# One layer of a hybrid mLSTM and attention backbone: the root of the mLSTM head norms as a power on GpSimd, and the last head's masks moved

## The chip, the cores and the metric

The kernel runs on one core of one Trainium2 chip. The metric is the device time of one execution in microseconds (us), the median of several runs. Engines: PE is TensorE's matrix multiply and PEld its weight load, DVE is VectorE, ACT is ScalarE, POOL is GpSimd, SP is SyncE, which issues the DMAs here.

## The reference, cut to what matters

One layer, 1024 latent tokens and 256 context tokens of width 1024. After a modulated norm and one input projection there are two groups of heads, a bidirectional mLSTM (4 heads of 128) and a windowed attention; their outputs are joined, projected, and followed by a gated convolutional mixer. The change lies in the mLSTM group:

```
d_log = cum[..., :, None] - cum[..., None, :] + li[..., None, :]
order = tril(ones((MLSTM_CHUNK, MLSTM_CHUNK)))
d_log = where(order, d_log, -inf)              # the mask
m_t = maximum(a_log, max(d_log, axis=-1))
dec = exp(d_log - m_t[..., None])              # the decay
s = einsum('bhntd,bhnsd->bhnts', q, k) * dec
...
def mlstm_merge(h, o, gain):                   # the head norm
    hn = h * rsqrt(mean(h * h, axis=-1) + EPS)
    return hn * gain * sigmoid(o)
```

## The kernel before

Tokens are worked on in blocks of 128: 2 context blocks (NC) and 8 latent blocks (NL). The four mLSTM heads (H = 4) go one after the other. While the recurrence of head h runs (`mlstm(h, ...)`), the dense projections of head h + 1 (`dense`) are interleaved with it, piece by piece: the outer loop takes one step of the recurrence and then as much dense work as a rate allows. Beside the last head there is no next one; there the query projections of attention (`qgen`, tile px) are interleaved, at a lower rate, and what is left of them runs after the head.

For one head, `mlstm` does the following.

- It loads `ee` (8 blocks of 128 x 2 x 128, both directions) by four broadcast DMAs from DRAM, two blocks each (`ee_load`, line 659). `ee` has one buffer, so the first load waits for the last use by the head before.
- Nine backward states, i = 0 to 8: transposes of the keys (line 665, tile pn, four buffers), two scaled copies on ScalarE (lines 669, 671), a product (line 692), and the state update on VectorE (line 700 for the first, 702 for the others), which releases pn. In between it adds the masks to `ee` (`mask(b)`, line 675; `mask(i - 2)` from i = 2, the last one with the first forward state) and takes the exponentials (`decay(b)`, line 679). At i = 7 the output gate is formed (lines 715, 716).
- Forward states and outputs by block: scores (line 734) times `ee` (line 737), forward state (722, 727), products with the states and values (745, 746, 748), division by the normaliser (751 to 760), and on line 763 a square with a running sum into `hss[:, b]`.
- `finish()`: a root of `hss` on ScalarE (796), its inverse on VectorE (797), and for each block the scale of the head's output into `ym` (799). For heads 0 to 2 it is a generator that the next head's backward states step through from i = 1 on (`next(fins[0])`): the root, the inverse and block 0 in the first step, a block in each later one. For the last head it runs whole at the end.

ScalarE's functions come from tables. Tanh (566, 715) and Exp (679, 1152) run without a reload between them; Sqrt needs another one. So each root brings a table load before it (at line 796) and another before the next Tanh or Exp (566 in heads 1 and 2, 679 in the last head, 1044 after it).

The order of work: in the stages of heads 0 to 2 (the recurrence of head h with the projections of head h + 1) the order on every engine is as written. In the stage of the last head only TensorE's order is as written; what VectorE, ScalarE, GpSimd and the DMA queue do is put in order by the framework's planner when the program is built, by its own estimates of when each instruction is ready, with the order of writing as the priority. After the last head, memory of the recurrence is freed and given to attention's tiles (`kT2`, `vv`, `wor`); an Exp on one element of `vv` (line 1044) and the loads of `vv`'s raw values (line 927, wor<-kv_d) come first there. GpSimd has no work between the input stage and attention.

Of the kernel before, what the change touches and what calls it, by code (L numbers as in the profile page):

```python
# [12 lines left out]
AF = mybir.ActivationFunctionType  # L13
ALU = mybir.AluOpType
# [9 lines left out]
NL = SEQ // P  # L24
NC = CTX // P
NCH = NL + NC
H = 4
DH = 128
# [6 lines left out]
EPS = 1e-6  # L35
# [43 lines left out]
def build(tc, I, out, dbg=None):  # L79
    nc = tc.nc  # L80
    dbg = dbg or {}
    V, S, G, T = nc.vector, nc.scalar, nc.gpsimd, nc.tensor
# [11 lines left out]
    eps_t = cp.tile([P, 1], F32, name="eps_t")  # L94

    def spc(n, i=0, w=1):
        a = SP[n][0] + i
        return sp[:, a:a + w]

    def rwc(n, i=0, w=None):  # L100
        a, b = RW[n]
        return rw[:, a + i:(b if w is None else a + i + w)]
# [81 lines left out]
    tri = xp.tile([P, 2, P], F32, name="tri", bufs=1)  # L184
# [458 lines left out]
            dump("kT", kT[:]); dump("qT", qT[:]); dump("va", va[:].rearrange("p c e -> p (c e)"))  # L643

    fins = []

    def mlstm(h, kT, qT, va):
        cbk = tp.tile([P, NL, DH + 1], F32, name="cbk", tag="cbk", bufs=1)
# [2 lines left out]
        hss = tp.tile([P, NL], F32, name="hss", tag="hss")  # L651
        g1 = lambda t, d, c: t[:, d, c, h:h + 1]
        yv = ym[:, :, h * DH:(h + 1) * DH]
        E1 = DH + 1


        ee = tp.tile([P, NL, 2, P], F32, name="ee", tag="ee", bufs=1)
        def ee_load(b):
            nc.sync.dma_start(ee[:, b:b + 2], m_d[:].rearrange("(c h) d t -> h c d t", h=H)
                              [h:h + 1, NC + b:NC + b + 2].broadcast_to([P, 2, 2, P]))  # L660

        ee_load(0)
        def tr(c):
            pn = pl.tile([P, 512], F32, name="pn", tag="l")
            T.transpose(pn[:, 0:P], kT[:, c * P:(c + 1) * P], ident[:])
            kwb = None
            if c != NC:
                kwb = tp.tile([P, DH], F32, name="kwb", tag="kwb", bufs=3)
                S.activation(kwb[:], pn[:, 0:P], AF.Copy, scale=g1(gw, 1, c))
            if c < NCH - 1:  # L670
                S.activation(kwf[:, c], pn[:, 0:P], AF.Copy, scale=g1(gw, 0, c))
            return pn, kwb

        def mask(b):
            V.tensor_tensor(out=ee[:, b], in0=ee[:, b], in1=tri[:], op=ALU.add)

        def decay(b):
            for d in range(2):
                S.activation(ee[:, b, d], ee[:, b, d], AF.Exp, bias=g1(a_, d, NC + b), scale=-1.0)
# [6 lines left out]
        for i, c in enumerate(order[1][:-1]):  # L686
            pn, kwb = ahead.pop(0)
            if i + 2 < NCH - 1:
                ahead.append(tr(order[1][i + 2]))
            elif i + 2 == NCH - 1:  # L690
                tr(order[1][i + 2])
            T.matmul(pn[:, P:P + E1], kwb[:], va[:, c], start=True, stop=True)
            if c == 1:
                nx = tp.tile([P, E1], F32, name="cst", tag="cst")[:]
            elif c == 0:
                nx = cbk[:, NL - 1]
            else:
                nx = cbk[:, c - NC - 1]
            if prev is None:
                V.tensor_copy(nx, pn[:, P:P + E1])  # L700
            else:
                V.scalar_tensor_tensor(out=nx, in0=prev, scalar=g1(gd, 1, c), in1=pn[:, P:P + E1],
                                       op0=ALU.mult, op1=ALU.add)
            prev = nx
            if i < 3:
                ee_load(2 * i + 2)
            if fins and i:
                next(fins[0])
            if i > 1:
                mask(i - 2)  # L710
            if i in (4, 6, 8):
                decay(i // 2 - 2)
            if i == TN:

                S.activation(yv, yv, AF.Tanh, scale=0.5)
                V.scalar_tensor_tensor(out=yv, in0=yv, scalar=1.0, in1=rwc("gain", h * DH, DH).unsqueeze(1)
                                       .broadcast_to([P, NL, DH]), op0=ALU.add, op1=ALU.mult)
            yield
        cf, cfs = [None], []

        def step(c, ps):
            T.matmul(ps, kwf[:, c], va[:, c], start=True, stop=True)
            nx = tp.tile([P, E1], F32, name="cst", tag="cst")
            if cf[0] is None:
                V.tensor_copy(nx[:], ps)
            else:
                V.scalar_tensor_tensor(out=nx[:], in0=cf[0], scalar=g1(gd, 0, c), in1=ps, op0=ALU.mult, op1=ALU.add)
            cf[0] = nx[:]
            cfs.append(nx[:])

        def first(c):
# [3 lines left out]
            if b:  # L735
                step(c - 1, pe[:, P:P + E1])
            V.scalar_tensor_tensor(out=ee[:, b], in0=pe[:, 0:P].unsqueeze(1).broadcast_to([P, 2, P]),
# [29 lines left out]
        for c in range(NC):  # L767
            pn = pl.tile([P, 512], F32, name="pn", tag="l")
            step(c, pn[:, 0:E1])
            if c == 0:  # L770
                cfs.clear()
            if c == 0:
                mask(NL - 1)
            decay(3 + c)
            yield
        first(NC)
# [16 lines left out]
        cfs.clear()  # L793

        def finish():
            S.activation(hss[:], hss[:], AF.Sqrt, bias=eps_t[:], scale=1.0 / DH)
            V.reciprocal(hss[:], hss[:])
            for b in range(NL):
                V.scalar_tensor_tensor(out=yv[:, b], in0=hid[:, b], scalar=hss[:, b:b + 1], in1=yv[:, b],
                                       op0=ALU.mult, op1=ALU.mult)  # L800
                if b < NL - 1:
                    yield
            fins.clear()
            yield
        if h < H - 1:
            fins.append(finish())
        else:
            for _ in finish():
                pass
# [179 lines left out]
    for h in range(H):  # L989
# [20 lines left out]
        with tc.manual_schedule(engines=order_):  # L1010
            dn = dense(h + 1, wkq, wvo, *nh) if nh else qgen()
            rate = RATE if nh else RATE3
            for n, _ in enumerate(mlstm(h, *cur)):
                if nh is None and n == LW3:
                    late()
                    rga = pq.tile([P, D], F32, name="rga", tag="rga")
                    nc.sync.dma_start(rga[:], row(0))
                if nh and n in (2, LW):
                    w = wnext((n // LW,))
                    if n == LW:  # L1020
                        wvo.append(w)
                        wnext = ahead_load(h + 2, 0)
                elif nh and n in (24, 27):
                    wkq = wnext((n // 27,))
                    if n == 27 and h + 2 < H:
                        wnext = ahead_load(h + 2, 1)
                elif nh and n >= 3 and n != 15:
                    next(ada, 0)
                debt += rate * (1 + (n == 0))
                while debt > 0:  # L1030
                    w = next(dn, None)
                    if w is None:
                        break
                    debt -= w
# [1003 lines left out]
    for t, (p, ps, fresh) in enumerate(products):  # L2038
        for j in range(NP):
# [35 lines left out]
            if NP + 3 <= n < NP + 3 + NL:  # L2075
                b = n - NP - 3
# [118 lines left out]
```

## Time and profile before

| | |
|---|---|
| median of 3 runs | 1264.26 us (1264.09 to 1265.34) |
| the profiled execution | 1263.85 us |
| its span | 1262.1 us |
| granted TensorE clock, mean | 0.999 |
| TensorE busy | 1233.2 us (98%) |
| VectorE busy | 973.4 us (77%) |
| ScalarE busy | 638.8 us (51%) |
| GpSimd busy | 187.5 us (15%) |
| ScalarE's table loads at line 796 | 4, 1283 ns each |

The span runs from the first to the last instruction of one profiled execution, the time of an execution also has what lies around it. Rows of a time line give the start in us, the duration in us, the engine, the line, the operation, out<-in, the shapes and the count of instructions that were merged; in brackets stands how long the engine was idle before it and what ended that wait. In the groups by line the columns are busy us and mean ns, then the idle time before them.

### The profile page before, as it was taken

Reading aid. Unit: us, or ns where it says so; the run is one execution under the profiler, and the core shown is the slowest. Engines: PE = TensorE matmul, PEld = TensorE weight load, DVE = VectorE, ACT = ScalarE, POOL = GpSimd, SP = SyncE. Lnnn points to the kernel's source line nnn. Section 1 sums busy time; section 2 is a strip of 40 time slices with the busy share of each in tenths; the row PEclk is TensorE's granted clock in tenths of the full one; section 3 lists DMA queues with packets and bytes.
Section 4 is the critical chain, followed back from the end, with each engine's and each line's share of the span. In section 5 each row is a group of like instructions: output and inputs, shape, how many; then the busy total and the mean of one; then the engine's idle time right before and its main releaser. Section 6 shows DMA issues by size and latency. Waiting matters only on the chain.

```text
span 1262.1 us, 19247 instructions
## 1 busy us (share of the span) xinstructions
PE 1233.2 (98%) x7044; PEld 1059.5 (84%) x7044; DVE 973.4 (77%) x1691; ACT 638.8 (51%) x1310; POOL 187.5 (15%) x162
## 2 busy tenths in 40 slices
PE   6999999999999999999999999999999999999997
PEld 4799999999898888888887888888888888788886
DVE  5863777777887888788987877777777777877887
ACT  6732556464865777776843333333333334434435
POOL 1200000000001444221002232133231232001000
PEclk9999999999999999999999999999999999999999
DMA  9541635352254333104314322223322237975563
GB/s 360 190 138 35 151 117 152 119 178 68 85 176 165 128 126 110 51 34 167 117 51 133 116 98 104 93 101 116 103 105 100 94 136 269 335 252 187 192 195 134
DMA packets 90560, 176.17 MB, mean 140 GB/s; under 512 B 12954, under 2 KB 29538, under 8 KB 90466
## 3 DMA queue, kind: packets, MB, share of 16 engines
q1 hardware_dynamic: 90178, 174.15, 41.1%
q8 instruction: 56, 0.92, 0.3%
q10 hardware_dynamic: 288, 0.79, 0.2%
q14 instruction: 38, 0.31, 0.1%
HBM read 136.58 MB, written 38.33 MB: 139 GB/s over the span
## 4 chain that ended last, share of the span: by engine, by line
PE 80%; DVE 7%; ACT 5%; DMA 5%; issue 2%; SPq 1%; POOL 1%; ACTq 0%; DVEq 0%; POOLq 0%
PE pd L2032 14%; PE pa L1492 8%; PE pc L1492 8%; PE pp L600 7%; PE pe L1492 4%; PE pd L1492 4%; PE pb L1492 4%; PE u L1194 3%; PE pv L305 2%; PE pv L307 2%; PE pv L306 2%; DMA wa<-in_w_ada_dram 2%; PE pt L1171 2%; PE po L305 2%; PE po L307 1%
## 5 line engine op out<-in xcount | busy, mean ns | idle before, releaser
L1609 ACT CAST wh<-Rb 128x1024 fp32r<-128x1024 f32 (+1 forms) x63 | 56.8, 903 | 144.4 <-PE pd L1492 77.3
L2032 PE MATMUL pd<-dh,al 128*128 128x512 f32 x296 | 115.4, 390 | 0.8 <-DVE al L1373 0.8
L2032 PE MATMUL pd<-dl,ah 128*128 128x512 f32 x296 | 115.3, 389 | 0.0
L2032 PE MATMUL pd<-dh,ah 128*128 128x512 f32 x296 | 115.2, 389 | 0.0
L1492 PE MATMUL pc<-hB,wh 128*128 128x512 f32 x344 | 105.5, 389 | 0.0
L1492 PE MATMUL pa<-hB,wh 128*128 128x512 f32 x336 | 103.7, 390 | 0.3 <-ACT sn L1691 0.2
L1210 DVE TENSOR_TENSOR wl<-Rb,wh 128x1024 fp32r<-128x1024 f32 (+1 forms) x63 | 65.8, 1046 | 39.2 <-ACT wh L1609 38.6
L1727 POOL TENSOR_TENSOR tt<-vt,tt 128x512 f32<-128x512 f32 x22 | 29.5, 1343 | 367.5 <-ACT tt L1721 367.5
L600 PE MATMUL pp<-hl,wh 128*128 128x512 f32 x256 | 79.3, 405 | 0.0
L305 PE MATMUL pv<-wh,hl 128*128 128x256 f32 x256 | 75.9, 296 | 0.0
L1492 PEld LDWEIGHTS pc<-hB,wh 128*128 128x128 f32 x344 | 64.6, 188 | 13.4
L1492 PEld LDWEIGHTS pa<-hB,wh 128*128 128x128 f32 x336 | 62.9, 188 | 14.0 <-ACT sn L1691 1.1
L307 PE MATMUL pv<-wh,hl 128*128 128x256 f32 x256 | 72.4, 283 | 0.0
L306 PE MATMUL pv<-wl,hl 128*128 128x256 f32 x256 | 72.3, 282 | 0.0
L1492 PE MATMUL pc<-hB,wl 128*128 128x512 f32 x172 | 66.4, 389 | 0.0
L2032 PEld LDWEIGHTS pd<-dh,al 128*128 128x128 f32 x296 | 55.6, 188 | 12.9 <-DVE al L1373 1.6
L2032 PEld LDWEIGHTS pd<-dl,ah 128*128 128x128 f32 x296 | 55.6, 188 | 12.0 <-DVE dl L1373 0.3
L1492 PE MATMUL pa<-hB,wl 128*128 128x512 f32 x168 | 65.4, 389 | 0.0
L2032 PEld LDWEIGHTS pd<-dh,ah 128*128 128x128 f32 x296 | 55.6, 188 | 11.6
L1178 ACT CAST ph<-pt 128x512 fp32r<-128x512 f32 (+1 forms) x88 | 46.2, 525 | 26.0 <-PE pt L1171 25.8
L1148 DVE TENSOR_REDUCE nm<-sps 128x1 f32<-128x641 f32 (+1 forms) x64 | 50.3, 786 | 4.9 <-PE sps L1144 3.4
L1492 PE MATMUL pd<-hB,wh 128*128 128x512 f32 x176 | 53.9, 390 | 0.0
(1095 smaller groups left out, 3692.1 us busy)
## 6 DMA issues: line engine op xcount, KB each, us to landing
w<-in_w_ada_dram SPq DMA_DIRECT2D x64, 256.0 KB, 2.7
br<-in_w_down_dram SPq DMA_DIRECT2D x25, 512.0 KB, 5.6
ar<-act_s SPq DMA_DIRECT2D x44, 256.0 KB, 3.2
Ra<-in_w_up_dram SPq DMA_DIRECT2D x21, 512.0 KB, 3.6
Rb<-in_w_up_dram SPq DMA_DIRECT2D x21, 512.0 KB, 3.6
act_a<-tt SPq DMA_DIRECT2D x33, 256.0 KB, 2.0
act_s<-tt SPq DMA_DIRECT2D x33, 256.0 KB, 2.0
wr<-in_w_h_dram SPq DMA_DIRECT2D x16, 512.0 KB, 5.1
```

The costliest lines, as they stand in the source:

```text
L305: T.matmul(ps, st_hi, mv_hi, start=first, stop=False)
L306: T.matmul(ps, st_hi, mv_lo, start=False, stop=False)
L307: T.matmul(ps, st_lo, mv_hi, start=False, stop=last)
L600: T.matmul(pp[:, 512 * n:512 * n + 512], wkq[sw][:, kt, cs], hl[n][part][:, kt, :], start=kt == 0 and sw + part == 0, stop=kt == KT - 1 an ...
L1148: V.tensor_reduce(out=self.nm[:, j:j + 1], in_=self.sv[j], axis=AX.X, op=ALU.max, negate=True)
L1178: S.copy(self.ph[i][:, :w], self.pt[i][:, :w])
L1194: T.matmul(self.u[:], vv[:, c, self.g], part[i][:, kk * 2 * P:(kk + 1) * 2 * P], start=kb + m == 0, stop=kb == last and m == 1)
L1210: sub = lambda e, o, x, y: e.tensor_tensor(out=o, in0=x, in1=y, op=ALU.subtract)
L1492: T.matmul(ps[:, cols], wt[sw][:, j, kt * P:kt * P + P], hB[part][:, blk, kt, cols], start=first and n == 0, stop=last and n == len(seq) - ...
L1609: S.copy(wt[0][:], src)
L1727: G.tensor_tensor(out=self.tt[:, h2_], in0=self.vt[:], in1=self.tt[:, h2_], op=ALU.mult)
L2032: T.matmul(ps[:], ac[sa][:, js], w[sw], start=first and n == 0, stop=last and n == 2, skip_group_check=not fresh)
```

## The change

The root and the inverse become two instructions on GpSimd: a multiply-add of `hss` (times 1/128, plus EPS), and a power with exponent -0.5, taken from a small constant tile. That constant is written once before the heads, over eight columns of `bsh_a`, a parameter that is not read any more by then. With it the Sqrt table is no longer needed by the four heads.

In the last head (`lag` = 3 instead of 1), masks are written two states later: `mask(i - 4)` from i = 4 on, and masks 5, 6 and 7 with the first forward state. Its masks of blocks 0 and 1 run on GpSimd instead of VectorE. In heads 0 to 2 the masks stay as they are.

```
     fins = []
+    G.memset(spc("bsh_a", 0, NL), -0.5)
...
+        lag = 1 if h < H - 1 else 3
...
         def mask(b):
-            V.tensor_tensor(out=ee[:, b], in0=ee[:, b], in1=tri[:], op=ALU.add)
+            e = G if lag > 1 and b < 2 else V
+            e.tensor_tensor(out=ee[:, b], in0=ee[:, b], in1=tri[:], op=ALU.add)
...
-            if i > 1:
-                mask(i - 2)
+            if i > lag:
+                mask(i - lag - 1)
...
-            if c == 0:
-                mask(NL - 1)
+            for b in (range(NL - lag, NL) if c == 0 else ()):
+                mask(b)
...
         def finish():
-            S.activation(hss[:], hss[:], AF.Sqrt, bias=eps_t[:], scale=1.0 / DH)
-            V.reciprocal(hss[:], hss[:])
+            G.tensor_scalar(out=hss[:], in0=hss[:], scalar1=1.0 / DH, scalar2=EPS, op0=ALU.mult, op1=ALU.add)
+            G.tensor_tensor(out=hss[:], in0=hss[:], in1=spc("bsh_a", 0, NL), op=ALU.pow)
```

## The prediction

> **What bounds the kernel now.** I read the page first, for the busy shares.
>
> ```profile
> span 1262.1 us, 19247 instructions
> PE 1233.2 (98%) x7044; PEld 1059.5 (84%) x7044; DVE 973.4 (77%) x1691; ACT 638.8 (51%) x1310; POOL 187.5 (15%) x162
> ```
>
> TensorE is busy for 1233.2 of 1262.1 us, so the change can win only where TensorE waits. The next view is the busy time by stretch (columns: PE, PEld, DVE, ACT, POOL, granted clock, DMA share, GB/s), around the last head, which runs from 320.7 to about 394 us.
>
> ```profile
> 300.00:320.00 20.00, 20.00 (x173) 20.00 (x172) 14.03 (x35) 11.31 (x35) 0.00 (x0) 1.00 0.03 10
> 320.00:340.00 20.00, 18.30 (x145) 16.68 (x144) 16.95 (x56) 17.88 (x54) 0.00 (x0) 1.00 0.38 107
> 340.00:360.00 20.00, 19.14 (x169) 18.91 (x168) 16.57 (x65) 14.70 (x45) 0.00 (x0) 1.00 0.21 73
> ```
>
> Up to 320 us TensorE has no idle time; between 320 and 360 us it idles 1.70 + 0.86 = 2.56 us, with VectorE and ScalarE fuller than before. GpSimd does nothing in any of the three, and the clock is at 1.00. So the size of any gain is about 2.6 us plus what stands behind 360 us, out of 1264.26: 0.2%, or 2.53 us, which is about what a measurement of this kernel can tell from no change.
>
> The third view is the chain of waits, with the start of each head's dense stage (first key matmuls) and the one extra block of TensorE work.
>
> ```profile
> 123.89 2.88 PE pc__1499 L592 x24
> 188.96 2.88 PE pc__2268 L592 x24
> 226.46 0.79 PE pq L831 x8
> 254.90 2.88 PE pc__3055 L592 x24
> ```
>
> Head 0's stage takes 188.96 - 123.89 = 65.07 us and has no norm of an earlier head to finish; head 1's takes 254.90 - 188.96 = 65.94 us and has one, besides the block of 0.79 us at 226.46. That leaves 0.08 us for a whole finish with its two table loads, root and inverse.
>
> **Part 1, the root in heads 0 and 1.** Each finish drops a table load, a root and an inverse, and the load that restores the table. ScalarE's order of time, and VectorE's row that comes after the inverse:
>
> ```profile
> 190.57 0.19 ACT L763 ACTIVATION_READ_ACCUMULATOR nm<-hid 128x1 f32 x1
> 197.24 1.28 ACT L796 ACT_TABLE_LOAD   x1
> 198.53 0.30 ACT L796 ACTIVATE hss<-hss,eps_t 128x8 f32<-128x8 f32 x1
> 199.10 0.35 DVE L799 SCALAR_TENSOR_TENSOR ym<-hid,hss,ym 128x128 f32<-128x128 f32 x1
> ```
>
> By the 0.08 us above this is worth nothing: all engines keep their order here, and TensorE has no gap to close. I put it at 0, with ends of 0 and -0.2 (two heads at 0.08). What covers the new work: the sums of squares are complete at 190.76, the scale on line 799 runs at 199.10, so the two GpSimd instructions have 8.3 us. If that cover were gone, line 799 would hold back VectorE's queue, with the state updates (line 702) behind it, and TensorE behind those.
>
> The Trainium skill, "ScalarE: Activation LUTs", section "What ACT_TABLE_LOAD costs", counts a drain of about 1.38 us on top of the load, about 2.66 us a switch. Here the root starts at 198.53, right where the load of 1.28 us ends, so this trace shows no drain in the price. By the page each removed load would free twice the ScalarE time; my sum would stay, since ScalarE does not set the end in it.
>
> What do the two GpSimd instructions cost? The page's groups have these rows.
>
> ```profile
> L908 POOL TENSOR_TENSOR wor<-wor,rga 128x512 f32<-128x512 f32 x8 | 10.3, 1288 | 2.5 <-DMA wor<-in_w_out_dram 2.5
> L2184 POOL MEMSET const-bfloat16-1.0<- 128x1 bf16 x1 | 0.1, 102 | 0.0
> ```
>
> On 8 elements a multiply-add should be near the memset, 0.1 us. No row has a power. From below it is 0.1 us, from above I take 1.8 us, more than any two-input row of its engine above; my value is 1.0 us, in the middle, as neither row is like it. The same memset row prices the new constant, once, on an engine that is idle: 0.
>
> **Part 2, the last head's front.** Three views of the same time: VectorE, ScalarE, TensorE.
>
> ```profile
> 322.12 0.35 DVE L760 SCALAR_TENSOR_TENSOR hid<-nm,dn,hid 128x128 f32<-128x128 f32 x1 [0.53 <-ACT hid L759]
> 323.80 0.76 DVE L675 TENSOR_TENSOR ee<-ee,tri 128x256 f32<-128x256 f32 x2 [1.32 <-DMA ee<-m_d]
> 324.47 0.29 DVE L700 COPY cst<-pn 128x129 f32<-128x129 f32 x1
> 325.02 0.76 DVE L675 TENSOR_TENSOR ee<-ee,tri 128x256 f32<-128x256 f32 x2 [0.26 <-DMA ee<-m_d]
> 325.70 0.34 DVE L702 SCALAR_TENSOR_TENSOR cbk<-cst,gd,pn 128x129 f32<-128x129 f32 x1
> 327.69 0.19 DVE L797 RECIPROCAL hss<-hss 128x8 f32<-128x8 f32 x1
> 327.80 0.30 DVE L702 SCALAR_TENSOR_TENSOR cbk<-cbk,gd,pn 128x129 f32<-128x129 f32 x1
> 339.00 0.43 DVE L752 TENSOR_TENSOR nm<-pi,nm 128x258 f32<-128x258 f32 x1 [0.32 <-PE pe L734]
> 341.05 1.23 DVE L157 TENSOR_TENSOR wl<-wr,wh 128x1024 fp32r<-128x1024 f32 x1 [0.23 <-ACT wh L156]
> 344.31 0.42 DVE L737 SCALAR_TENSOR_TENSOR ee<-pe,ee 128x256 f32<-128x256 f32 x1
> ```
>
> ```profile
> 324.63 1.28 ACT L796 ACT_TABLE_LOAD   x1
> 328.56 1.28 ACT L679 ACT_TABLE_LOAD   x1
> ```
>
> ```profile
> 324.82 0.33 PE L665 MATMUL pn<-ident,kT 128*128 128x128 f32 x1 [0.43 <-DVE cst L700]
> 330.38 0.33 PE L665 MATMUL pn<-ident,kT 128*128 128x128 f32 x1 [0.30 <-DVE cbk L702]
> 331.11 0.49 PE L692 MATMUL pn<-va,kwb 128*128 128x129 f32 x2 [0.40 <-ACT kwf L671]
> 344.87 0.35 PE L745 MATMUL pj<-cst,qT 128*128 128x129 f32 x1 [0.86 <-DVE ee L737]
> ```
>
> VectorE waits for the broadcast loads of ee: 1.32 us before blocks 0 and 1 and 0.26 us before blocks 2 and 3. From 325.02 on its rows follow without a gap but for 0.32 and 0.23 us until line 737 at 344.31, which releases TensorE's longest stall, 0.86 us. So from 325.02 to 344.7 VectorE's list of work sets the time. What ScalarE or TensorE get done earlier in between only moves TensorE's stall to 344.
>
> *Blocks 0 and 1 to GpSimd.* VectorE loses 324.47 - 323.80 = 0.67 us of masks ahead of the first state's copy (line 700), and the copy no longer waits for the load. TensorE's 0.43 us at 324.82 goes. What is late next: masks 2 and 3, which wait for the second load until 325.02 and stand ahead of line 702.
>
> *The lag.* In the text of the kernel before, masks 2 and 3 belong to states 4 and 5, yet they sit ahead of state 1's update (325.70). The planner, not the text, put them there, because VectorE had nothing else ready. Writing them two states later leaves them as ready as before, so I expect them in the same place: 0. At the other end they go behind, and VectorE is free of the waits and of the moved masks: 1.32 + 0.67 + 0.26 = 2.25 us. I stay with 0, since the planner has already moved them three states forward. On GpSimd a mask has half the elements of line 908's row, so about 0.65 to 1.29 us; both are done by 326.4, and block 0 is first read by ScalarE's exponential, behind the load at 328.56. Masks 5 to 7 end up after the first forward state, the same work in the same stretch: 0.
>
> *The inverse* leaves VectorE at 327.69: the next row starts 0.11 us later, so -0.1. *The two gaps* of 0.32 and 0.23 us may close when TensorE and ScalarE are ahead: between 0 and -0.55, I take -0.3. *The two table loads* are 2.56 us of ScalarE; the second stands in the chain ahead of TensorE's stalls at 330.38 and 331.11 (0.70 us). With VectorE as the bound they give 0, at most -0.7.
>
> **Part 3, the last head's end.** ScalarE, VectorE, TensorE:
>
> ```profile
> 356.12 0.20 ACT L763 ACTIVATION_READ_ACCUMULATOR nm<-hid 128x1 f32 x1
> 357.94 0.30 ACT L796 ACTIVATE hss<-hss,eps_t 128x8 f32<-128x8 f32 x1
> ```
>
> ```profile
> 358.69 2.18 DVE L799 SCALAR_TENSOR_TENSOR ym<-hid,hss,ym 128x128 f32<-128x128 f32 x8
> ```
>
> ```profile
> 371.93 0.51 PE L895 MATMUL pt<-identr,qs 128*128 128x128 f32 x4 [0.38 <-DVE qs L890]
> ```
>
> The sums are ready at 356.32, the root at 358.24. On GpSimd 0.1 + 1.0 us give the power at 357.4, up to 0.8 us sooner. The eight scales free the room into which the values of attention are loaded, and the chain leads through those loads and VectorE to TensorE's 0.38 us at 371.93. I take -0.3, between 0 and -0.38. The load for Exp after it goes too, under query projections that keep TensorE busy: 0.
>
> **Sum.** 0 - 0.1 - 0.3 - 0.3 = -0.7 us. The profiled execution took 1263.85 us (span 1262.1 and 1.75 around it), so 1263.15; it lies 0.41 us under the median of the runs, 1264.26, which makes the forecast 1263.5 us.
>
> **Rivals.** *The lag works* (masks 2 and 3 leave the head of VectorE's list): -0.7 - 2.25 = -2.95 us, which is also all of the 2.56 + 0.38 us that TensorE idles: 1261.3. For it: the longest waits of the front are these loads. Against: those two masks ran ahead of the text before.
>
> *The ports.* Two VectorE groups of the same operation and size differ where GpSimd works beside one of them:
>
> ```profile
> L1210 DVE TENSOR_TENSOR Rb<-Rb,Ra 128x512 f32<-128x512 f32 x21 | 32.0, 1525 | 0.7
> L1210 DVE TENSOR_TENSOR Rb<-Ra,Rb 128x512 f32<-128x512 f32 x42 | 28.1, 710 | 0.0
> ```
>
> That is 0.82 us for one instruction. If GpSimd's two masks slip to where VectorE adds masks 2 and 3, each holds one of them up by as much: at most 1.6 us, and about 1.1 with half-sized masks; the forecast becomes 1264.6, no change. Against: the first load lands at 323.80, when VectorE has nothing to mask. The Trainium skill, "SBUF — State Buffer", section "SBUF: two separate sides", says that a VectorE instruction with two SBUF inputs and a GpSimd one exclude each other for a whole instruction; the two rows agree with it.
>
> *The power is slow.* From 356.32 it may take 1.9 us before it is later than the root; past that each us delays the scales, the loads and the stall at 371.93 one for one. At 6 us the loss there is about 4.1 us and the result 1264.26 - 0.4 + 4.1 = 1268.0, slower; it becomes a measurable loss from about 4.8 us on. The 8.3 us of heads 0 and 1 would still cover it. For it: no row prices the power. Against: no GpSimd instruction of the rows above goes past 1.3 us, with 512 elements and not 8.
>
> **Chances.** The forecast 0.50, on its own 1262.5 to 1264.3; the lag works 0.22; the ports 0.15; the slow power 0.07; another order of VectorE's or the DMA queue's work through the planner, either way, 0.06. Faster by over 0.2% means under 1261.7: two thirds of the second case and half of the last, 0.18. Slower means over 1266.8: 0.07, with the slow power. Within: 0.75. The range, 1261.0 to 1265.4, leaves out the slow power, a third of the lag's case and some of the last.
>
> **What would show it.** Right: TensorE at 100% and the stage lengths of heads 0 and 1 unchanged; no table load at lines 679 and 1044; line 700 near 322.9; masks 2 and 3 still waiting for their load ahead of the first line 702; a stall at line 745 that remains. Wrong: line 702 ahead of all VectorE masks; VectorE masks of about 1 us; a wait for GpSimd at line 799.

## The result: slower by 0.4%

| | before | after |
|---|---|---|
| median of 6 runs each, same chip | 1264.38 us | 1268.99 us |
| ratio, 95% interval | | 1.0038 (1.0028 to 1.0048) |
| the profiled execution, its span | 1262.1 us | 1267.2 us |

The forecast was 1263.5 us and no change; the change costs 4.6 us. The head of the page after:

```profile
span 1267.2 us, 19257 instructions
PE 1234.8 (97%) x7044; PEld 1059.8 (84%) x7044; DVE 972.4 (77%) x1685; ACT 628.0 (50%) x1298; POOL 196.5 (16%) x173
```

VectorE and ScalarE have 1.0 and 10.8 us less work, as the change wants, GpSimd has 9.0 us more, and the span is 5.1 us longer. TensorE's busy time, with the same 7044 matmuls, is only 1.6 us higher, so most of the loss is waiting. The window in which most of it stands:

```profile
320.00:340.00 20.00, 15.30 (x122) 14.08 (x121) 14.57 (x45) 14.39 (x47) 3.29 (x4) 1.00 0.42 107
```

Between 320 and 340 us TensorE idles 4.70 us where it idled 1.70. The second measure is a shift: the start of each TensorE instruction less that of the same one in the kernel before, as the median over a stretch. From 40 to 318 us it is 0.10 us and constant (this shift of the start differs from kernel to kernel below, from -0.27 to 1.51 us). From 324 to 327 us it falls by 0.6 to 0.9, a gain; by 345 to 358 us it is 2.10 us above the start (the **front** of the last head), by 392 to 420 us another 1.94 (the **end**), and by 1150 us another 1.01. These three make the 5.1 us with the start. Heads 0 and 1, by the starts of the same key matmuls in the chain of waits after:

```profile
123.99 2.88 PE pc__1500 L592 x24
189.06 2.88 PE pc__2269 L592 x24
255.00 2.88 PE pc__3056 L592 x24
```

The stages are 65.07 and 65.94 us long, to the hundredth what they were.

What the new instructions cost, by the groups after (busy us and mean ns):

```profile
L800 POOL TENSOR_TENSOR hss<-hss,sp 128x8 f32<-128x8 f32 x4 | 6.6, 1649 | 0.3
L799 POOL TENSOR_SCALAR hss<-hss 128x8 f32<-128x8 f32 x4 | 0.8, 200 | 227.4 <-DMA w<-in_w_ada_dram 132.2 <-ACT nm L766 95.1
L678 POOL TENSOR_TENSOR ee<-ee,tri 128x256 f32<-128x256 f32 x2 | 1.4, 740 | 65.5 <-ACT kwb L671 65.5
```

A power is 1.65 us and a mask 0.74, inside the bounds of the prediction (0.1 to 1.8 and 0.65 to 1.29); a multiply-add is 0.20, twice what it was put at. No new instruction is far from its price; what the 1.65 us of the power cost where they stand is tested below. Line numbers after are those of before plus 2 for lines 665 to 671 and plus 3 behind them (675 is 678, 702 is 705, 737 is 740, 745 is 748, 799 is 802, 908 is 911). The kernels below that keep a root in some heads have four lines more behind line 801 (802 is 806, 893 is 897, 911 is 915).

The front after, first GpSimd and VectorE (start, duration, engine, line; in brackets the wait):

```profile
324.28 1.44 POOL L678 TENSOR_TENSOR ee<-ee,tri 128x256 f32<-128x256 f32 x2 [65.45 <-ACT kwb L671]
325.80 0.20 POOL L799 TENSOR_SCALAR hss<-hss 128x8 f32<-128x8 f32 x1
326.08 1.65 POOL L800 TENSOR_TENSOR hss<-hss,sp 128x8 f32<-128x8 f32 x1
```

```profile
323.00 0.29 DVE L703 COPY cst<-pn 128x129 f32<-128x129 f32 x1 [0.43 <-PE pn L695]
324.52 0.35 DVE L705 SCALAR_TENSOR_TENSOR cbk<-cst,gd,pn 128x129 f32<-128x129 f32 x1
327.76 0.35 DVE L802 SCALAR_TENSOR_TENSOR ym<-hid,hss,ym 128x128 f32<-128x128 f32 x1 [2.90 <-POOL hss L800]
328.03 0.34 DVE L705 SCALAR_TENSOR_TENSOR cbk<-cbk,gd,pn 128x129 f32<-128x129 f32 x1
331.64 0.42 DVE L678 TENSOR_TENSOR ee<-ee,tri 128x256 f32<-128x256 f32 x1
335.75 1.21 DVE L157 TENSOR_TENSOR wl<-wr,wh 128x1024 fp32r<-128x1024 f32 x1
338.22 0.41 DVE L740 SCALAR_TENSOR_TENSOR ee<-pe,ee 128x256 f32<-128x256 f32 x1
```

The first state is copied at 323.00, as foretold, and VectorE's first mask comes only at 331.64, behind six state updates: the lag has moved the masks. But the planner gave GpSimd the two masks first and head 2's power behind them. The masks' load is issued at 320.22 and takes 3.6 us to land, and the masks start at 324.28 (the bracket names a copy of ScalarE that ended just ahead of that; with the masks alone, in run e2, it names the load). And the planner put the scale of line 802 ahead of the second state update. VectorE stands for 2.90 us with that update behind it. ScalarE and TensorE in the same time:

```profile
331.27 1.05 ACT L156 CAST wh<-wr 128x1024 fp32r<-128x1024 f32 x1 [1.00 <-DMA wr<-in_w_q_dram]
332.23 0.36 ACT L671 ACTIVATE kwb<-pn,gw 128x128 f32<-128x128 f32 x1
```

```profile
328.43 0.33 PE L667 MATMUL pn<-ident,kT 128*128 128x128 f32 x1 [1.87 <-DVE cbk L705]
332.90 0.49 PE L695 MATMUL pn<-va,kwb 128*128 128x129 f32 x2 [0.64 <-ACT kwf L673]
338.69 0.71 PE L751 MATMUL pi<-va,ee 128*128 128x129 f32 x4 [1.59 <-DVE ee L740]
```

A second thing is new on ScalarE, the place of the cast of attention's query weight (line 156). ScalarE and VectorE before:

```profile
332.04 0.37 ACT L671 ACTIVATE kwf<-pn,gw 128x128 f32<-128x128 f32 x1
334.05 1.05 ACT L156 CAST wh<-wr 128x1024 fp32r<-128x1024 f32 x1
```

```profile
334.67 0.43 DVE L737 SCALAR_TENSOR_TENSOR ee<-pe,ee 128x256 f32<-128x256 f32 x1
335.13 1.22 DVE L157 TENSOR_TENSOR wl<-wr,wh 128x1024 fp32r<-128x1024 f32 x1
```

The cast ran at 334.05 before, behind all scaled copies of the backward states; now it stands ahead of the last one's (332.23) and waits for its load. The load is not later: it is issued at 325.44 and takes 5.7 us to land, against 325.32 and 5.9 us before. And on VectorE the cast's other half (line 157, 1.21 us) now stands ahead of the first score multiplication, line 740, for which TensorE waits 1.59 us.

The end after, ScalarE's last sum, GpSimd, VectorE, TensorE:

```profile
358.63 0.20 ACT L766 ACTIVATION_READ_ACCUMULATOR nm<-hid 128x1 f32 x1
```

```profile
359.19 1.64 POOL L800 TENSOR_TENSOR hss<-hss,sp 128x8 f32<-128x8 f32 x1
```

```profile
360.87 2.19 DVE L802 SCALAR_TENSOR_TENSOR ym<-hid,hss,ym 128x128 f32<-128x128 f32 x8 [1.87 <-POOL hss L800]
376.44 1.23 DVE L911 TENSOR_TENSOR wor<-wor,rga 128x1024 f32<-128x1024 f32 x1 [0.42 <-DMA wor<-in_w_out_dram]
378.74 1.23 DVE L911 TENSOR_TENSOR wor<-wor,rga 128x1024 f32<-128x1024 f32 x1 [0.41 <-DMA wor<-in_w_out_dram]
```

```profile
374.87 0.52 PE L898 MATMUL pt<-identr,qs 128*128 128x128 f32 x4 [0.59 <-DVE qs L893]
382.91 0.50 PE L898 MATMUL pt<-identr,qs 128*128 128x128 f32 x4 [1.00 <-DVE qs L893]
```

Before, VectorE had a query to rotate while the root ran:

```profile
357.95 0.42 DVE L317 TENSOR_TENSOR ta<-px,rope 128x256 f32<-128x256 f32 x1 [0.87 <-PE px L307]
358.40 0.38 DVE L317 TENSOR_TENSOR z<-px,rope 128x256 f32<-128x256 f32 x1
```

Now it waits 1.87 us for the power, and later two scalings of w_out stand close together, each waiting for its load, ahead of the rest of a query (line 893) for which TensorE waits. One wait of 0.38 us has become 0.59 and 1.00.

### The profile page after: what moved, and what is told of

It is laid out like the page before. It is cut to its first block, busy times and chain, and to the rows that moved or that the text cites. A ratio compares the mean times of both kernels' runs of the same rounds, so it can differ in the third digit from the quotient of the medians.

```text
span 1267.2 us, 19257 instructions
## 1 busy us (share of the span) xinstructions
PE 1234.8 (97%) x7044; PEld 1059.8 (84%) x7044; DVE 972.4 (77%) x1685; ACT 628.0 (50%) x1298; POOL 196.5 (16%) x173
## 4 chain that ended last, share of the span: by engine, by line
PE 77%; DVE 9%; ACT 5%; DMA 5%; issue 2%; SPq 1%; POOL 1%; DVEq 0%; ACTq 0%; POOLq 0%
PE pd L2035 12%; PE pa L1495 8%; PE pc L1495 8%; PE pp L600 7%; PE pe L1495 4%; PE pd L1495 4%; PE pb L1495 4%; PE u L1197 3%; PE pv L305 2%; PE pv L307 2%; PE pv L306 2%; PE pt L1174 2%; PE po L305 2%; PE po L307 1%; PE po L306 1%
```

## The experiments

Each kernel was measured in 5 rounds beside the kernel before. An engine's **list** is the order of its instructions. The shifts are those of the one profiled execution, each stretch less the one ahead of it; the last column is VectorE's wait for GpSimd at the scales of the last head's own end. "Late" is everything behind 420 us; where it is large it arises mostly between 600 and 630 us; half of the change's comes at 1070.

How far a shift of one execution can be trusted, the kernels with equal lists show. e14 and e15 have the change's list on every engine and on the DMA queue: their late parts are 0.19 and 0.11 us where the change has 1.01 (e10 and e16, again with one list, have 2.75 and 1.11), so much of "late" is scatter between executions. Up to the last head's end e15 is the change, instruction for instruction, and its front is 3.17 where the change has 2.10; e2 and e3, equal up to there as well, are 0.07 us apart.

| kernel | median, before | ratio (95%) | front | end | late | wait at end |
|---|---|---|---|---|---|---|
| the change | 1268.99, 1264.38 | 1.0038 (1.0028, 1.0048) | 2.10 | 1.94 | 1.01 | 1.87 |
| e1 power alone | 1268.64, 1264.56 | 1.0029 (1.0018, 1.0040) | 0.58 | 1.51 | 2.71 | 1.87 |
| e2 masks alone | 1265.05, 1264.56 | 1.0005 (0.9996, 1.0014) | -0.88 | 1.21 | 0.33 | none |
| e4 root at the end | 1268.13, 1264.56 | 1.0034 (1.0021, 1.0046) | 2.17 | 0.79 | 1.30 | none |
| e5 power first in GpSimd's queue | 1269.61, 1264.56 | 1.0040 (1.0028, 1.0053) | 2.28 | 2.44 | 0.05 | 1.88 |
| e3 root in the front | 1266.19, 1264.91 | 1.0012 (1.0003, 1.0021) | -0.81 | 2.69 | 0.39 | 1.96 |
| e9 power in heads 0, 1 alone | 1265.74, 1264.91 | 1.0006 (0.9997, 1.0015) | 0.18 | 0.41 | 0.33 | none |
| e10 the change, late cast | 1270.52, 1264.91 | 1.0042 (1.0030, 1.0055) | 1.93 | 2.16 | 2.75 | 1.87 |
| e11 e9 with masks, later cast | 1264.12, 1264.91 | 0.9996 (0.9988, 1.0005) | -1.02 | -0.18 | 0.84 | none |
| e12 e3, later cast | 1267.47, 1264.79 | 1.0019 (1.0010, 1.0027) | -1.05 | 2.78 | 2.17 | 1.82 |
| e13 e1, late cast | 1266.50, 1264.79 | 1.0013 (1.0004, 1.0022) | -0.41 | 1.83 | 0.15 | 1.88 |
| e14 product for power, front | 1269.91, 1264.79 | 1.0039 (1.0027, 1.0051) | 2.77 | 1.59 | 0.19 | 1.88 |
| e15 product for power, end | 1267.39, 1264.55 | 1.0023 (1.0014, 1.0032) | 3.17 | 0.98 | 0.11 | 0.44 |
| e16 e10, product in the front | 1266.96, 1264.55 | 1.0018 (1.0009, 1.0027) | -0.56 | 1.58 | 1.11 | 1.88 |

**First: which part costs, and where.** The power alone (all masks on VectorE, no lag):

```
-        lag = 1 if h < H - 1 else 3
+        lag = 1
-            e = G if lag > 1 and b < 2 else V
+            e = V
```

> The root as a power on GpSimd for all four heads, masks as in the kernel before. Theory Q (GpSimd's queue: the power of head 2 stands behind masks that wait for their load, and VectorE's scale on line 802 waits 2.90 us for it): without masks on GpSimd the power of head 2 starts at about 323.5 us, is done by 325.4, VectorE waits under 1 us, and the front loss of 2.1 us shrinks to under 1; the loss behind 360 us (2.0) stays if it comes with the last root, so about 1266.5 to 1267.5. Rival P (the removed table loads shift the planner's lists on VectorE and ScalarE, whatever GpSimd does first): front and end lose as in the changed kernel, about 1269.

```profile
337.70 0.71 PE L751 MATMUL pi<-va,ee 128*128 128x129 f32 x4 [2.09 <-DVE ee L740]
```

It is slower by 0.29%, most of the change's loss, though in its profile front and end make only 2.09 us and late makes 2.71. VectorE waits only 0.65 us at line 802 of the front, since GpSimd has no masks ahead of the power; yet line 157 stands ahead of line 740 here too, TensorE waits 2.09 us there, and the end loses 1.51 us.

The masks alone (root and inverse as before):

```
-            G.tensor_scalar(out=hss[:], ...)
-            G.tensor_tensor(out=hss[:], ..., op=ALU.pow)
+            S.activation(hss[:], hss[:], AF.Sqrt, bias=eps_t[:], scale=1.0 / DH)
+            V.reciprocal(hss[:], hss[:])
```

> Masks as in the changed kernel (blocks 0 and 1 on GpSimd, lag 3), root and inverse on ScalarE and VectorE as before. Theory Q: no power, so no wait for GpSimd; line 700 comes at about 323.0, TensorE gains the 0.6 to 0.8 us that the changed kernel had at 326 us, nothing is lost behind 360: 1263 to 1264.5. Rival M (the moved masks are the harm, by the ports or by pressing VectorE later): the front still loses about 2 us, 1266 or more.

No difference that can be told. The front gains 0.88 us and the end gives it back. By themselves GpSimd's masks and the lag are not the loss; yet beside the power they turn a front of 0.58 into one of 2.10 us. Why, the second group of runs shows.

Root and inverse back in the last head's own finish alone (`if h != H - 1:` ahead of the power):

> The changed kernel, but the last head's own finish keeps root and inverse on ScalarE and VectorE; the other three finishes use the power. Theory E (the 2.0 us behind 360 us come with the last root's move, through other lists of VectorE and the DMA queue): they go, about 1267.0, and the front loss of 2.1 us stays. Rival (the end only inherits the shift of the front): 1269, with TensorE still losing about 2 us between 362 and 383 us.

The front is that of the change (2.17), the end loses 0.79 instead of 1.94, and the whole is still slower, by more than the 1267.0 expected: two losses, in two places. And in the finish of head 2 alone, the one that runs in the front (`if h != H - 2:`):

> The changed kernel, but the finish of head 2 (which runs in the last head's front) keeps ScalarE's root and VectorE's inverse; heads 0, 1 and the last head's own finish use the power, masks 0 and 1 stay on GpSimd and the lag stays. Its list of VectorE's instructions up to 345 us is that of the run with the masks alone. Theory 'the lists' (the front's loss comes from head 2's power: its place in GpSimd's queue behind the masks, and the other VectorE list that it brings about): the front gains about 0.9 us against before, as in the run with the masks alone, no wait for GpSimd at line 802 of the front, and TensorE's wait for the first line 740 is under 1 us; the end loses between 1 and 2 us; in all 1265 to 1266. Rival 'the masks' (GpSimd's masks or the lag cost the front its time): the front stays 2 us behind, 1268 to 1269.

The front turns from a loss of 2.10 into a gain of 0.81 us, with GpSimd's masks, the lag and three powers kept. The front's loss comes with the power of head 2 and what the planner does about it. The end lost 2.69, more than foreseen.

The power in heads 0 and 1 alone, the rest as before:

> The power in heads 0 and 1 alone; heads 2 and 3 finish with the root and the inverse, all masks on VectorE, no lag. VectorE's list is that of the kernel before without two inverses. Theory 'the first heads are free': no shift of TensorE beyond the start's jitter, 1264.3 to 1264.8, ratio within 0.001 of 1. Rival 'the power costs wherever it stands' (a quarter of the loss for each finish): 1265.6 to 1267.

The ratio's interval takes in 1 and the shift is constant from 40 to 318 us: no cost there is seen. The median lies 0.8 us above that of before, outside the 1264.3 to 1264.8 expected; by the shifts it comes from the front and the end (0.59) and late (0.33), although VectorE's list there is that of before. Its size stays unexplained; it is too small for the measurement.

**Second: what holds the front.** GpSimd's instructions of the last head in the order written, so that the power runs ahead of the masks:

```
-        order_ = {mybir.EngineType.PE}
+        order_ = {mybir.EngineType.PE, mybir.EngineType.Pool}
```

> The changed kernel with GpSimd's order as written in the last head too, so that head 2's power comes ahead of the two masks; VectorE's list is the same. Theory Q: the power runs at about 323.7 to 325.4, VectorE's wait at line 802 falls from 2.90 to about 0.5 us, and TensorE gets back 1 to 2 us of the 2.1 lost up to 345 us: 1267 to 1268. The masks end later, near 327, and ScalarE's exponentials may wait for them about 1 us. Rival P: the order on GpSimd does not matter, 1269.

VectorE's wait falls from 2.90 to 1.38 us, and the front does not move (2.28). The rows of GpSimd and VectorE:

```profile
324.93 0.97 POOL L799 TENSOR_SCALAR hss<-hss 128x8 f32<-128x8 f32 x1 [64.69 <-ACT nm L766]
327.58 1.46 POOL L678 TENSOR_TENSOR ee<-ee,tri 128x256 f32<-128x256 f32 x2
327.65 0.80 DVE L802 SCALAR_TENSOR_TENSOR ym<-hid,hss,ym 128x128 f32<-128x128 f32 x1 [1.38 <-POOL hss L800]
```

Now the masks are late, and ScalarE waits 1.62 us for them. That could hide the gain, so a cleaner probe was needed: a product in place of head 2's power, which leaves the root out for that head. Every engine's list stays the same, and only one duration changes (1.65 us to 0.20).

```
-            G.tensor_tensor(..., op=ALU.pow)
+            G.tensor_tensor(..., op=ALU.pow if h != H - 2 else ALU.mult)
```

> The changed kernel, but head 2's finish multiplies by the constant where it took the power (the root is left out for that head, so ym's third quarter is scaled wrongly). Every engine's list is that of the changed kernel, instruction for instruction; only the price of one GpSimd instruction changes, from 1.65 us to about 0.2 to 0.3 us. Theory 'the wait at 802 sets the front': VectorE's wait at line 802 falls from 2.90 to about 1.5 us and the front's loss from 2.1 to 0.7 us; 1267.4 to 1267.9. Rival 'the list ahead of line 740 sets it': TensorE stands better up to 334 us, the stall at line 740 grows by as much, and the front stays 2 us behind, 1269.

VectorE, ScalarE and TensorE of this run:

```profile
327.01 0.35 DVE L802 SCALAR_TENSOR_TENSOR ym<-hid,hss,ym 128x128 f32<-128x128 f32 x1 [1.81 <-POOL hss L800]
332.19 1.04 ACT L156 CAST wh<-wr 128x1024 fp32r<-128x1024 f32 x1 [2.68 <-DMA wr<-in_w_q_dram]
333.81 0.49 PE L695 MATMUL pn<-va,kwb 128*128 128x129 f32 x2 [2.30 <-ACT kwf L673]
339.61 0.71 PE L751 MATMUL pi<-va,ee 128*128 128x129 f32 x4 [1.61 <-DVE ee L740]
```

My theory fell: VectorE waits 1.1 us less, and the front gains nothing (it is 0.67 us later, which is within the scatter above). The rival was no nearer: the stall at line 740 did not grow (1.61 us). The time went into a third place, ScalarE's cast, which now waits 2.68 us for the load of the query weight with the last state's copies behind it. In five runs with this list on ScalarE and VectorE the cast's start tells the front:

| | cast starts, less the start's shift | front | difference |
|---|---|---|---|
| the change | 331.27 - 0.10 = 331.17 | 2.10 | 329.07 |
| e4 | 331.60 - 0.40 = 331.20 | 2.17 | 329.03 |
| e5 | 332.86 - 1.51 = 331.35 | 2.28 | 329.07 |
| e14 | 332.19 - 0.43 = 331.76 | 2.77 | 328.99 |
| e15 (below) | 332.13 - 0.03 = 332.10 | 3.17 | 328.93 |

The front follows the landing of a load, to 0.14 us, whatever GpSimd does; the cast is a gate, a point behind which nothing starts earlier. The load's time differs by itself: the change and e15 both issue it at 325.44, and it takes 5.7 us to land in the one and 6.6 us in the other. Taking this gate away: the second weight one step later (`LW3 = 13` for 12), which puts the cast behind the last state's copies and line 157 behind the first line 740.

> The changed kernel, but the second query weight's load and casts are written one step later (LW3 = 13 instead of 12), so that VectorE's subtraction of line 157 (1.21 us) stands behind the first score multiplication (line 740) and not ahead of it; line 893 and the rotation stay ahead. Theory 'the lists': TensorE's wait of 1.59 us for the first line 740 falls by about 1.2, to 0.4 us, the wait of 2.90 us for GpSimd at line 802 stays, and the front's loss falls from 2.1 to about 0.9 us; 1267.5 to 1268.2 unless the end's list moves too. Rival 'one delay, seen twice' (the front is late because of the wait at 802 alone, and the stall at 740 is only where it shows): the stall moves to another instruction and the front stays 2 us behind, 1269.

```profile
328.86 0.35 DVE L802 SCALAR_TENSOR_TENSOR ym<-hid,hss,ym 128x128 f32<-128x128 f32 x1 [3.37 <-POOL hss L800]
333.66 1.04 ACT L156 CAST wh<-wr 128x1024 fp32r<-128x1024 f32 x1
339.03 0.71 PE L751 MATMUL pi<-va,ee 128*128 128x129 f32 x4 [0.80 <-DVE ee L740]
```

The cast no longer waits, the stall at 740 halves, and the front still loses 1.93: of the two waits the one at line 802 is left, 3.37 us in this run, and TensorE waits 2.34 us for the update behind it. By itself neither cure helps, so both together, the late cast and the product:

> The changed kernel with the second query weight one step later (LW3 = 13; ScalarE's cast of line 156 then stands behind the last state's scalings, and VectorE's line 157 behind the first line 740), and with a product in place of head 2's power (the root is left out for that head). Its lists are those of the run with LW3 = 13 alone, whose front lost 1.93 us with a wait of 3.37 us at line 802. Theory 'two gates, the later one counts' (GpSimd's power at line 802, and the load of w_q ahead of ScalarE's cast; taking away one alone left the front 1.9 to 2.8 us behind): with both gone the front loses 0.3 to 0.9 us. Rival 'something else sets 345 us' (VectorE's order around line 740): the front stays at 1.5 us or more. In all 1267.5 to 1269, since the end still loses 2 us.

```profile
327.20 0.35 DVE L802 SCALAR_TENSOR_TENSOR ym<-hid,hss,ym 128x128 f32<-128x128 f32 x1 [1.46 <-POOL hss L800]
332.49 1.05 ACT L156 CAST wh<-wr 128x1024 fp32r<-128x1024 f32 x1 [1.32 <-DMA wr<-in_w_q_dram]
336.40 0.71 PE L751 MATMUL pi<-va,ee 128*128 128x129 f32 x4 [0.76 <-DVE ee L740]
```

With the lists of the run before and one shorter instruction, the front goes from a loss of 1.93 to a gain of 0.56 us, more than the theory asked. Two gates, and the later one counts: shown. (The cast waits here as well, but behind the last state's copies; what it holds up are exponentials.) Moving the weight moves the cast and line 157 together, so not all of the 3.33 us between e14 and e16 need be the cast's. What line 157 costs by itself, the next run shows. The late cast with the power and without GpSimd's masks, where the wait at 802 is short:

> The power in all four heads without GpSimd's masks and without the lag, and the second query weight one step later (LW3 = 13), so that line 157 stands behind the first line 740. With line 157 ahead the same kernel waited 0.65 us for GpSimd at line 802 and 2.09 us for the first line 740, and its front lost 0.57 us. Theory 'the list ahead of line 740 costs its own time where the wait at 802 is short': the stall falls to about 0.9 us and the front gains 0.6 us against before. Rival 'VectorE's sum of work sets 345 us whatever its order': the front stays at a loss of 0.5 us. The end loses 1 to 2 us as long as two scalings of w_out follow each other in VectorE's list; in all 1266.5 to 1268.5.

```profile
336.63 0.71 PE L751 MATMUL pi<-va,ee 128*128 128x129 f32 x4 [0.95 <-DVE ee L740]
```

The stall at 740 falls from 2.09 to 0.95 us and the front from a loss of 0.58 to a gain of 0.41. So where neither gate holds, the place of line 157 has its own price, about 1 us by this one pair.

**Third: the end.** A product for the power of the last head, which leaves its root out, with the change's lists kept:

> The changed kernel, but the last head's own finish multiplies by the constant where it took the power (the root is left out for that head, so ym's last quarter is scaled wrongly). Every engine's list stays that of the changed kernel. In the changed kernel the last head's scales (line 802) end at 363.06, and the loads of the attention's values and of w_out follow from there; net of the front's 2.1 us that is within 0.1 us of the kernel before, and still the end loses 2.0 us. Theory 'the list waits for the loads': with the power cheaper by 1.4 us the scales and the loads come 1.4 us sooner, the waits for w_out at the two scalings (0.42 and 0.41 us) go, and the end's loss falls from 2.0 to between 0.4 and 1.2 us; 1267.5 to 1268.3. Rival 'the list alone' (VectorE's two scalings of 1.2 us stand ahead of the query's rest whether or not their loads are there): the end still loses 1.6 us or more, 1268.6 to 1269.4.

```profile
360.43 1.67 DVE L802 SCALAR_TENSOR_TENSOR ym<-hid,hss,ym 128x128 f32<-128x128 f32 x6 [0.44 <-POOL hss L800]
378.81 1.23 DVE L911 TENSOR_TENSOR wor<-wor,rga 128x1024 f32<-128x1024 f32 x1 [1.44 <-DMA wor<-in_w_out_dram]
```

The end's loss falls from 1.94 to 0.98, as expected (the change, e5 and e14 have the same list and lose 1.94, 2.44 and 1.59, so some 0.6 to 1.5 us are the power's); but one thing went the other way: the wait for w_out at the second scaling did not go, it grew to 1.44 us. What is left I put down to this list, which the run does not show by itself. Run e3 shows the same pair at its worst, VectorE and then TensorE:

```profile
376.91 1.23 DVE L915 TENSOR_TENSOR wor<-wor,rga 128x1024 f32<-128x1024 f32 x1 [1.45 <-DMA wor<-in_w_out_dram]
381.08 0.52 PE L902 MATMUL pt<-identr,qs 128*128 128x128 f32 x4 [2.05 <-DVE qs L897]
```

A list with the last head's power and the pair taken apart (e3 with `LW3 = 14`):

> The power in heads 0, 1 and in the last head's own finish, root and inverse in head 2, masks 0 and 1 on GpSimd with the lag, and the second query weight two steps later (LW3 = 14). By its list the two scalings of w_out at the end (line 911 of the changed kernel) have a query's rest (line 893) between them again, as in the kernel before; the last head's power is unchanged. Theory 'the end's list': the front gains 0.8 us or more, the waits for line 893 at 371 and 379 us fall from 0.64 and 2.05 us to under 1 us together, and the end loses under 0.5 us; 1263.2 to 1264.5. Rival 'the power of the last head costs the end': it loses 1 to 2 us as before, 1265.5 or more.

The waits for the query's rest at 371 and 379 us are gone, as the theory said, and the end still loses 2.78 us: the total, 1267.47 us, is the rival's. It has a new stall instead, because a copy of attention's values now stands ahead of the rotation of a query and waits for ScalarE:

```profile
362.91 0.83 DVE L938 TENSOR_TENSOR vv<-wor,vv 128x640 fp32r<-128x640 f32 x1 [1.82 <-ACT vv L937]
365.69 0.36 PE L305 MATMUL px<-wh,hl 128*128 128x256 f32 x1 [1.70 <-DVE z L317]
```

Last, masks and lag kept, root and inverse in heads 2 and 3, a later cast:

> The power in heads 0 and 1, root and inverse in heads 2 and 3, masks 0 and 1 on GpSimd with the lag, and the second query weight two steps later (LW3 = 14). Theory 'the lists': the front gains 0.9 us or more as in the run with the masks alone; its list of the end is another one, so the end keeps the gain or gives back up to 1.2 us: 1263.2 to 1264.9. Rival 'GpSimd's masks cost the end': it gives the gain back whatever the list, 1265 or more.

The best of all, 1264.12 us, and its interval still takes in 1; its front and end together gain 1.20 us by the shifts, and late takes 0.84 of it. This kernel differs from e12 only in the last head's finish, and its end gains 0.18 us where that of e12 loses 2.78. The copy that waited 1.82 us there stands behind eleven instructions after the scales here, and not six, and waits 0.31:

```profile
364.31 0.83 DVE L938 TENSOR_TENSOR vv<-wor,vv 128x640 fp32r<-128x640 f32 x1 [0.31 <-ACT vv L937]
```

Over all fourteen kernels: with the power in the last head's finish the end loses 1.5 to 2.8 us, with the cheap product 0.98, with the root -0.2 to 1.2. But e11 shows that the wait is not the cause by itself: there VectorE waits 1.76 us for ScalarE's root ahead of its inverse, as long as it waits for GpSimd elsewhere, and the end loses nothing:

```profile
357.70 0.20 DVE L804 RECIPROCAL hss<-hss 128x8 f32<-128x8 f32 x1 [1.76 <-ACT hss L803]
```

So some 0.6 to 1.5 us of the end's loss go with the power's duration, by one run. That the rest goes with the order that the planner gives VectorE there is argued from the lists, of which two harmful forms were seen; no run has the power with the order that the root's lists have. That, and the late part beyond its scatter, stays open.

## Why the prediction was wrong

*Part 1, heads 0 and 1 are worth 0.* Right: stage lengths unchanged, no shift, and e9 agrees. The cover of 8.3 us took 0.20 + 1.65 us with ease.

*The prices.* The multiply-add was put near 0.1 us and took 0.20; the power was taken at 1.0 us between 0.1 and 1.8 and took 1.65; the masks 0.74, between 0.65 and 1.29. The power was mis-sized by 0.65 us; with a product of 0.20 us in its place the end lost 0.6 to 1.5 us less (e15).

*The lag is worth 0, because the planner has already moved masks 2 and 3.* This step failed outright. They left the head of VectorE's list (331.64). The rival built on that gave 2.25 us; the runs show a gain of 0.8 to 1.05 us for masks and lag in the front (e2, e3, e11, e12). What came next was closer behind than 2.25 us: in e3 TensorE then waits 0.82 us for a state's copy on ScalarE (line 673) and 0.65 us for line 740.

*"VectorE's list of work sets the time from 325 to 344.7", hence two table loads less are worth 0, at most -0.7.* This is the step that failed and lost the case. I priced the removed instructions as time on their engines, with both ends of the range at or below nothing, and took the order around them as given. But behind head 2 the order is the planner's. With the root and its two loads gone it moved the weight's half on VectorE ahead of the scores (e1), and with the lag also the cast on ScalarE ahead of the last state's copies: a load that nobody waited for became a gate of the front. In place of 0 to -0.7 us the front lost 2.10 us. That the planner did so because its estimates had ScalarE free earlier is argued, not shown. "Another order through the planner" had a chance of 0.06 and no place; it was what happened, twice.

*Head 2's finish on GpSimd.* I walked the cover of heads 0 and 1 and of the last head, and for head 2 only took the inverse off VectorE. GpSimd's queue was never walked in the front: masks waiting until 324.28, then the power until 327.73. Even so it would have been ready by 328.01, where line 799 stood before; but the new list has that scale at 324.86, ahead of the second state update. What the power costs there shows once the cast is out of the way: with a product for it the front is 2.49 us earlier (e10 to e16).

*Part 3, -0.3.* From the end of the last sum to the first scale it took 358.69 - 356.32 = 2.37 us before and 360.87 - 358.83 = 2.04 after: 0.33 us gained, where I had up to 0.8. That this is near the -0.3 of the sum is chance, since that term was bounded by the stall of 0.38 us behind it; and the end as a whole lost 1.94. What I did not count is that VectorE used to rotate a query while it waited (0.42 + 0.38 us) and now stands idle for 1.87 us with that work behind it.

*The other side.* The slow power was my only rival that ended clear of noise on the slow side, and I let it begin at 4.8 us. A power of 1.65 us, inside my bounds, was enough, with a queue in front of it and a state update behind it.

Of the three signs named for "wrong" two were there: line 705 ahead of all VectorE masks, and a wait for GpSimd at line 802. VectorE masks of about 1 us were not (0.42). The first state's copy came as foretold (323.00, less the start's 0.10). The stall at the line that was 745 remained in part (0.29 us at 347).

## What to carry to other kernels

Where a planner orders the engines, an edit's price has two terms: the instructions it adds or removes, and the new order, which can pull work that waits for a load ahead of work on the critical path. The second was larger here and of the other sign, so leave a range for it wherever the edit touches a part that the planner orders. Before work is moved to an idle engine, write down that engine's queue at that place: an idle engine with one waiting instruction ahead is not idle. And when one wait is taken away and nothing moves, look for a second gate behind it and take both away before the first is called innocent.

## What was unexpected in the hardware

- A power of 128 x 8 elements on GpSimd took 1.65 us each time, more than a two-input multiply of 128 x 512 elements on the same engine (1.29 us): the count of elements does not price it.
- A GpSimd multiply-add of 128 x 8 took 0.20 us alone and 0.97 us where it met VectorE's two-input instruction of 1.22 us (run e5). In the same run VectorE's scale took 0.80 us beside a GpSimd mask, and 0.35 elsewhere. The Trainium skill, "SBUF — State Buffer", section "SBUF: two separate sides", tells of such an exclusion, and these rows agree with it.
- The load of the query weight, issued at the same time in two executions of the same list, took 5.7 us to land in the one (the change) and 6.6 in the other (e15). Where an engine waits for it with critical work behind, that alone moved TensorE's front by 1.07 us.
